# Two-layer hybrid decoder trunk on one core: branch products of the mixer in the score banks, two priorities, and three attention branches some pieces later

## The chip, the cores and the metric

The kernel runs on one core of a Trainium2 chip. The metric is device time in microseconds (us), the median of the runs shown. The engines are PE (TensorE), DVE (VectorE), ACT (ScalarE), POOL (GpSimd) and SP (SyncE, which issues the loads of weights). Matmul results land in PSUM, which is eight banks; a bank holds 512 float32 columns for each of 128 partitions.

## The reference

Two layers. Each is a SwiGLU feed-forward (FFN), a token mixer and a second FFN; after each of the three, `x = LayerNorm(ALPHA * x + (1 + gate) * F(modulate(x)))`. There are 256 tokens of width 1024. The mixer is the part that the change touches, cut to what matters:

```python
proj = u @ w_in                       # queries, keys, values of A, B, C, D; index; gate logits
y_a = dilated_window_attention(...)   # 3 groups x 2 heads, softmax
y_b = dsa_attention(...)              # top-64 keys of an index score, then softmax, 4 heads
y_c = stick_breaking_attention(...)   # 4 heads: exp(log_sigmoid(z) + reversed cumulative sum)
y_d = forgetting_attention(...)       # 4 heads: softmax of q k + a cumulative sum of log f
gates = sigmoid(g_logit + b_gate).reshape(b, t, 4, D)
merged = sum(gates[:, :, i] * (branches[i] @ w_branch[i]) for i in range(4))
return merged @ w_out
```

## The kernel before

**Matmuls.** Every float32 product is three passes over float32r halves: a weight is loaded as `raw`, ACT casts it to `hi` (L262), DVE subtracts to get `lo` (L267), and PE runs hi by hi, hi by lo and lo by hi (`split_mm`, L286 to L288 with the weight stationary, L290 to L292 with the activations stationary).

**Order.** The code is straight-line Python. A planner at build time turns it into one queue for each engine: it goes by program position, and takes the earliest instruction that its own model of time says is ready, so that a later matmul can be put ahead of one that would wait. `tc.high_priority(offset=n)` moves the instructions inside it n positions ahead in that ranking. On the chip each queue runs in its fixed order.

**The mixer as pieces.** A `tick()` follows each piece of projection work, and `plan()` hangs the attention steps on tick numbers with `on(n, step)`. Ticks 15 to 18 follow the four pieces of a value projection. From tick 23 on the gate projections run in sixteen groups, one for each of 4 branches and 4 pairs of output blocks (`gates(bi, (pr,))`, two ticks each, one per half); after each but the first comes the product of the group before (`branch(bi, pr)`) and one tick. So group g has the ticks 3g+22 and 3g+23, and the branch product of group g-1 stands ahead of tick 3g+24. The branches come in the order A, C, D, B.

**PSUM.** Three rings of banks: `mm` (2 banks, projections), `acc` (4 banks, `acc_bank()`: scores, sums of C, outputs `y` of attention, the final output) and `tp` (2 banks, `tp_bank()`: transposes, and here the branch products). A ring's bank is taken again when the last reader of its former content is done.

**Steps.** `c_scores(j)` makes two heads' scores of C in two `acc` banks each; DVE adds the mask (L923). `c_logs` is one long chain over all of C's scores: ACT (L931 to L933), DVE (L934), `lf` on POOL, `eh` on ACT (L938), `el` on DVE (L939). `c_sums(j)` (L949 to L952) reads `eh` and `el` into the two `acc` banks x and y, which DVE subtracts (L954, L955); ACT takes the exponential (L956). `d_scores(j)` needs eight small tiles `lb` that POOL makes from `lf` (L968), two `acc` banks (L971, L972, then L744) and ends in a softmax (DVE L789, ACT L791 and L795). `pair_pt` transposes the probabilities of two heads into two `tp` banks (L749 to L751), and ACT copies each to `pt` (L753). `pair_pv` multiplies by the values into one `acc` bank (L762, L765); `y_out` splits that into halves (ACT L778, DVE L779). `a_pt` and `a_pv` do the same for A (copy L899, product L905).

**Merging.** `branch` multiplies gate and product on DVE (L1069 for A, L1071 for the others) and adds to `merged` (L1073, on POOL for C and D, on DVE for B). After B the merged block is cast to `mh` (ACT L1077) and its remainder to `ml` (DVE L1078), and `out` multiplies by the output weights.

Of the kernel before, what the change touches and what calls it, by code (L numbers as in the profile page):

```python
# [11 lines left out]
F32 = mybir.dt.float32  # L12
F32R = mybir.dt.float32r
BF16 = mybir.dt.bfloat16
AF = mybir.ActivationFunctionType
ALU = mybir.AluOpType
PSUM = bass.MemoryType.PSUM

D = 1024
# [67 lines left out]
MP = (0,1,0,0)  # L87
RP = 500
PP = 500
CS = 3  # L90
CVV = 4
NA0 = 0,1,3
NA1 = 0,2
FREE = 4
# [50 lines left out]
def trunk(ctx: ExitStack, tc: tile.TileContext, x, xT, crow, ada0, adac, adab, w_in0, w_in0x, gcol, bcol, ln_g, ln_b,  # L145
          w_in, w_out, mpair, mv0, mv12, mbrA, mbr, mwo, bgate, bforget, eye, rot, masks, out):
    nc = tc.nc
# [22 lines left out]
    def acc_bank():  # L170
        return pacc.tile([P, 512], F32, tag="acc", name="acc")
# [4 lines left out]
    def tp_bank():  # L176
        return ptp.tile([P, 512], F32, tag="tp", name="tp")
# [70 lines left out]
    def load(*srcs):  # L248

        widths = [src.shape[-1] for src in srcs]  # L250
        halves = [n if n <= 1024 else n // 2 for n in widths]
        parts = [[] for _ in srcs]
        for o in range(2):
            for src, n, half, got in zip(srcs, widths, halves, parts):
                if o * half >= n:
                    continue
                with tc.high_priority(offset=HP):
                    raw = wp.tile([P, 1024], F32, tag="raw", bufs=RB, name="raw")
                    nc.sync.dma_start(raw[:, :half], src[:, o * half:(o + 1) * half])
                    hi, lo = w_pair()  # L260
                    with behind() if held["free"] <= 0 < held["left"] else ExitStack():
                        nc.scalar.copy(hi[:, :half], raw[:, :half])  # L262
                        if held.get("pool_lo"):
                            held["pool_lo"] -= 1
                            nc.gpsimd.tensor_sub(lo[:, :half], raw[:, :half], hi[:, :half].bitcast(F32))
                        else:
                            held["lo"] = nc.vector.tensor_sub(lo[:, :half], raw[:, :half], hi[:, :half].bitcast(F32)).ins  # L267
                    held["left"] -= 1
                    held["free"] -= 1
                    got.append((hi, lo))  # L270

        def getter(half, got):
            def get(off, w):
                hi, lo = got[off // half]
                off %= half
                return hi[:, off:off + w], lo[:, off:off + w]
            return get

        gets = [getter(h, g) for h, g in zip(halves, parts)]
        return gets[0] if len(gets) == 1 else gets  # L280

    def split_mm(ps, w, xh, xl, start, stop, w_stationary=True):

        wh, wl = w
        if w_stationary:
            nc.tensor.matmul(ps, lhsT=wh, rhs=xh, start=start, stop=False)  # L286
            nc.tensor.matmul(ps, lhsT=wh, rhs=xl, start=False, stop=False)  # L287
            nc.tensor.matmul(ps, lhsT=wl, rhs=xh, start=False, stop=stop)  # L288
        else:
            nc.tensor.matmul(ps, lhsT=xh, rhs=wh, start=start, stop=False)  # L290
            nc.tensor.matmul(ps, lhsT=xh, rhs=wl, start=False, stop=False)  # L291
            return nc.tensor.matmul(ps, lhsT=xl, rhs=wh, start=False, stop=stop).ins  # L292
# [346 lines left out]
    def mixer(l, u, nxt, steps):  # L639
# [12 lines left out]
        def on(n, *fs):  # L652
            turns.setdefault(n, []).extend(fs)

        def tick():
            at["n"] += 1
            for f in turns.pop(at["n"], []):
                f()
# [87 lines left out]
        def transposed(p0, p1):  # L746

            ps = tp_bank()
            nc.tensor.transpose(ps[:, 0:128], p0, ident)  # L749
            nc.tensor.transpose(ps[:, 128:256], p1[:, 0:128], ident)  # L750
            nc.tensor.transpose(ps[:, 256:384], p1[:, 128:256], ident)  # L751
            pt = sp.tile([P, 384], F32, tag="pt", bufs=PTB, name="pt")
            nc.scalar.copy(pt, ps[:, :384])  # L753
            return pt

        def pv(y, heads):
# [48 lines left out]
        def head_pt(p):  # L805
            return transposed(p[:, 0:128], p[:, 128:384])
# [79 lines left out]
        def a_blocks(t):  # L886

            return [(g, h, kt) for g in range(3) for kt in range(t + 1) for h in range(2)]

        def a_pt(t):  # L890
            blocks, p = a_blocks(t), live["A"]
            live["Ap"] = []
            for i in range(0, len(blocks), 3):
                ps = tp_bank()
                for b, (g, h, kt) in enumerate(blocks[i:i + 3]):
                    c = (h * 3 + g) * 128 * (t + 1) + kt * 128
                    nc.tensor.transpose(ps[:, b * 128:b * 128 + 128], p[:, c:c + 128], ident)
                pt = sp.tile([P, 384], F32, tag="pt", bufs=PTB, name="pt")
                nc.scalar.copy(pt, ps[:, :384])  # L899
                live["Ap"] += [pt[:, b * 128:b * 128 + 128] for b in range(3)]  # L900

        def a_pv(t):
# [74 lines left out]
        def plan():  # L977

            f = lambda g, *a: (lambda: g(*a))
            for n, h in ((A0T, 0), (A0T + AST, 1)):  # L980
                on(n, f(a_scores, h))
                on(n + 3, f(a_pt, h))
                on(n + 4, f(a_pv, h))
            on(IK, index_keys)
            for h in range(4):
                on(IK + 3 + h, f(index_scores, h))
            for n in range(IK + 7, IK + 23):
                on(n, f(topk, 1))
            on(IK + 24, chosen)
            for j in range(2):  # L990
                on(15 + j, f(c_scores, j))
            on(16, c_logs)
            for j in range(2):
                on(20 + CS + j, f(c_sums, j))
            for j in range(2):
                on(23 + CVV + j, f(pair_pv, "C", j, 3))
                on(26 + 6 * j, f(d_scores, j))
                on(38 + 6 * j, f(b_scores, j))
                on(29 + 6 * j, f(pair_pt, "D", j))
                on(30 + 6 * j, f(pair_pv, "D", j, 5))  # L1000
                on(41 + 6 * j, f(pair_pt, "B", j))
                on(42 + 6 * j, f(pair_pv, "B", j, 1))
            for n, t in enumerate(STEPS):
                on(t, step)
            for n, piece in enumerate(held["affine"]):
                def late(piece=piece):
                    with tc.issue_after(held["lo"]):
                        piece()
                on(AM + n, late)
# [5 lines left out]
        for i in range(3):  # L1015
            for j, p in enumerate(proj(mpair[l, i], 2)):
                (qa if 2 * i + j < 3 else ka).append(rope(p, "qa", -0.125) if 2 * i + j < 3 else rope(p, "ka"))
        at["n"] = 0
        plan()
        iq = [rope(p, "iq") for p in proj(mpair[l, 3], 2)]  # L1020
        vproj([mv0[l, 0], mv0[l, 1]], 456, 0, extra=72)
# [30 lines left out]
        def branch(bi, pr):  # L1052

            b, last = BR_ORDER[bi], bi == 3
            k0, nk = KO[b]
            if pr == 0:
                src = mbrA[l] if b == 0 else mbr[l, b - 1]
                wb[bi] = load(src.rearrange("p a b -> p (a b)"))
            ps = tp_bank()
            for j in range(2):  # L1060
                m = pr * 2 + j
                for k in range(nk):
                    split_mm(ps[:, j * 256:(j + 1) * 256], wb[bi](k * D + m * 128, 128), ys[k0 + k][0], ys[k0 + k][1],
                             k == 0, k == nk - 1)
            tick()
            t = tg[bi, pr].rearrange("p a b -> p (a b)")
            mg = merged[:, 2 * pr:2 * pr + 2].rearrange("p a b -> p (a b)")
            if bi == 0:
                nc.vector.scalar_tensor_tensor(mg, t, 1.0, ps, op0=ALU.add, op1=ALU.mult)  # L1069
            else:  # L1070
                nc.vector.scalar_tensor_tensor(t, t, 1.0, ps, op0=ALU.add, op1=ALU.mult)  # L1071
                eng = nc.vector if last else nc.gpsimd
                eng.tensor_tensor(mg, mg, t, op=ALU.add)  # L1073
            if last:
                hslice = mh[:, 2 * pr:2 * pr + 2].rearrange("p a b -> p (a b)")
                lslice = ml[:, 2 * pr:2 * pr + 2].rearrange("p a b -> p (a b)")
                nc.scalar.activation(hslice, mg, AF.Copy, scale=0.5)  # L1077
                nc.vector.scalar_tensor_tensor(lslice, mg, 0.5, hslice.bitcast(F32), op0=ALU.mult, op1=ALU.subtract)  # L1078


        todo = []
# [9 lines left out]
        while turns:  # L1091
            tick()
        branch(*todo.pop(0))

        accs = [acc_bank() for _ in range(4)]
# [96 lines left out]
```

## Time and profile before

| | before |
|---|---|
| median of 3 runs | 1311.38 us (1308.73 to 1312.22) |
| the profiled execution's own time | 1315.82 us |
| its span, first to last instruction | 1314.0 us |
| PE busy | 1265.7 us (96%) |
| DVE, ACT, POOL busy | 1036.5, 652.6, 142.8 us |
| granted TensorE clock, mean | 0.998 |
| mixer of layer 0, of layer 1 (about) | 215 to 465 us, 860 to 1110 us |

Busy time of PE counts overlapped matmuls, so 96% doesn't say that PE runs at its peak; the distances between the starts of matmuls, and the waits, say where it lost time.

### The profile page before, as it was taken

What the parts mean: (1) busy time and instruction counts of PE and PEld (TensorE: products, weight loads), DVE (VectorE), ACT (ScalarE), POOL (GpSimd) and SP (SyncE); (2) the same over time, 40 slices, a digit from 0 to 9 for tenths busy, and PEclk for the clock granted to TensorE, in tenths of its full rate; (3) what the DMA queues carried; (4) which work ended last, traced back from release to release, by engine and by line L of the source; (5) the groups of instructions that cost most, each with busy time, mean ns of one, the idle gap of its engine ahead of it and who ended that gap; (6) DMA issues with size and microseconds to landing.
All of it is one profiled execution on the core that took longest, in us unless ns stands there. A gap on an engine that the chain in (4) does not pass through costs nothing.

```text
span 1314.0 us, 23415 instructions
## 1 busy us (share of the span) xinstructions
PE 1265.7 (96%) x9178; PEld 1175.6 (89%) x9178; DVE 1036.5 (79%) x1701; ACT 652.6 (50%) x1023; POOL 142.8 (11%) x150
## 2 busy tenths in 40 slices
PE   6999999999999999999999999999999999999997
PEld 5989888989989889998989999899989898899995
DVE  7788887888786799877698877688878768976565
ACT  4554355447564554444355444354666545554440
POOL 0130000214222000000000000012060210100000
PEclk9999999999999999999999999999999999999999
DMA  9889893756665639887548987457476655585530
GB/s 341 324 285 313 302 306 141 255 185 223 225 235 181 227 127 319 302 277 262 175 147 312 311 282 248 128 171 239 163 248 232 222 182 175 215 315 193 187 135 33
DMA packets 85847, 300.42 MB, mean 229 GB/s; under 512 B 10604, under 2 KB 12316, under 8 KB 85736
## 3 DMA queue, kind: packets, MB, share of 16 engines
q1 hardware_dynamic: 84392, 298.00, 66.3%
q8 instruction: 72, 1.18, 0.4%
q10 hardware_dynamic: 576, 0.60, 0.1%
q0 software_dynamic: 768, 0.32, 0.1%
q14 instruction: 39, 0.32, 0.1%
HBM read 297.81 MB, written 1.07 MB: 227 GB/s over the span
## 4 chain that ended last, share of the span: by engine, by line
PE 43%; issue 19%; DMA 16%; DVE 15%; ACT 5%; POOL 1%; DVEq 0%; ACTq 0%; SPq 0%; POOLq 0%
PE mm L286 9%; PE mm L287 8%; PE mm L288 8%; DVE lo L267 6%; DMA raw<-in_w_in_dram 5%; DMA raw<-in_adac_dram 5%; PE acc L290 3%; PE acc L292 3%; PE acc L291 3%; ACT hi L262 3%; DMA raw<-in_w_out_dram 3%; DVE raw L308 3%; DMA raw<-in_mpair_dram 1%; PE tp L286 1%; PE mm L290 1%
## 5 line engine op out<-in xcount | busy, mean ns | idle before, releaser
L267 DVE TENSOR_TENSOR lo<-raw,hi 128x1024 fp32r<-128x1024 f32 (+2 forms) x421 | 508.1, 1222 | 161.3 <-ACT hi L262 159.2
L262 ACT CAST hi<-raw 128x1024 fp32r<-128x1024 f32 (+1 forms) x422 | 433.8, 1040 | 322.3 <-PE mm L287 126.9
L286 PE MATMUL mm<-uh,hi 128*128 128x256 f32 x2032 | 574.7, 283 | 5.3 <-DVE h L525 3.1
L287 PE MATMUL mm<-ul,hi 128*128 128x256 f32 x2032 | 571.2, 281 | 0.0
L288 PE MATMUL mm<-uh,lo 128*128 128x256 f32 x2032 | 570.6, 281 | 0.0
L286 PEld LDWEIGHTS mm<-uh,hi 128*128 128x128 f32 x2032 | 383.0, 189 | 12.2 <-issue 5.3
L287 PEld LDWEIGHTS mm<-ul,hi 128*128 128x128 f32 x2032 | 383.5, 189 | 1.3
L288 PEld LDWEIGHTS mm<-uh,lo 128*128 128x128 f32 x2032 | 383.1, 189 | 0.3
L308 DVE CUSTOM_DVE_ANT_0 raw<-raw,cond_row,adab 128x1024 f32<-128x1024 f32 x128 | 163.9, 1292 | 47.1 <-DMA raw<-in_adac_dram 47.0
L290 PE MATMUL acc<-hi,hh 128*128 128x512 f32 x352 | 140.6, 400 | 2.2 <-ACT hh L531 1.7
L291 PE MATMUL acc<-lo,hh 128*128 128x512 f32 x352 | 139.1, 395 | 0.8 <-DVE lo L267 0.8
L292 PE MATMUL acc<-hi,hl 128*128 128x512 f32 x352 | 137.6, 396 | 0.1
L290 PEld LDWEIGHTS acc<-hi,hh 128*128 128x128 f32 x352 | 66.1, 188 | 17.7 <-ACT hh L531 3.3
L531 ACT CAST hh<-h 128x256 fp32r<-128x256 f32 x82 | 33.2, 405 | 97.4 <-DVE h L525 95.7
L292 PEld LDWEIGHTS acc<-hi,hl 128*128 128x128 f32 x352 | 65.9, 187 | 17.1 <-DVE hl L532 0.6
L291 PEld LDWEIGHTS acc<-lo,hh 128*128 128x128 f32 x352 | 66.1, 188 | 15.0 <-DVE lo L267 1.1
L408 POOL TENSOR_TENSOR rstd<-rstd,nhalf 128x1 f32<-128x1 f32 x12 | 7.6, 634 | 479.8 <-DVE rstd L407 479.8
L532 DVE TENSOR_TENSOR hl<-h,hh 128x256 fp32r<-128x256 f32 x74 | 31.2, 421 | 12.6 <-ACT hh L531 12.6
L290 PE MATMUL acc<-hi,uh 128*128 128x256 f32 (+1 forms) x128 | 38.7, 303 | 1.5 <-ACT uh L436 1.4
L1073 POOL TENSOR_TENSOR merged<-merged,tg 128x512 f32<-128x512 f32 x16 | 24.8, 1548 | 135.7 <-DVE tg L1071 57.2
L286 PE MATMUL tp<-y,hi 128*128 128x256 f32 x112 | 33.2, 297 | 5.8 <-ACT pt L753 5.7
L292 PE MATMUL acc<-hi,ul 128*128 128x256 f32 (+1 forms) x128 | 38.3, 299 | 0.0
(242 smaller groups left out, 1519.7 us busy)
## 6 DMA issues: line engine op xcount, KB each, us to landing
raw<-in_w_in_dram SPq DMA_DIRECT2D x174, 512.0 KB, 5.5
raw<-in_adac_dram SPq DMA_DIRECT2D x128, 512.0 KB, 5.4
raw<-in_mpair_dram SPq DMA_DIRECT2D x104, 512.0 KB, 4.9
raw<-in_w_out_dram SPq DMA_DIRECT2D x88, 512.0 KB, 5.3
ada<-in_ada_dram SPq DMA_DIRECT2D x16, 512.0 KB, 6.7
raw<-in_mwo_dram SPq DMA_DIRECT2D x16, 512.0 KB, 4.5
raw<-in_mv_dram SPq DMA_DIRECT2D x16, 384.0 KB, 3.8
raw<-in_mbr_dram SPq DMA_DIRECT2D x12, 512.0 KB, 3.8
```

What stands on the lines that cost most here:

```text
L262: nc.scalar.copy(hi[:, :half], raw[:, :half])
L267: held["lo"] = nc.vector.tensor_sub(lo[:, :half], raw[:, :half], hi[:, :half].bitcast(F32)).ins
L286: nc.tensor.matmul(ps, lhsT=wh, rhs=xh, start=start, stop=False)
L287: nc.tensor.matmul(ps, lhsT=wh, rhs=xl, start=False, stop=False)
L288: nc.tensor.matmul(ps, lhsT=wl, rhs=xh, start=False, stop=stop)
L290: nc.tensor.matmul(ps, lhsT=xh, rhs=wh, start=start, stop=False)
L291: nc.tensor.matmul(ps, lhsT=xh, rhs=wl, start=False, stop=False)
L292: return nc.tensor.matmul(ps, lhsT=xl, rhs=wh, start=False, stop=stop).ins
L308: nc.vector.tensor_tensor_reduce(raw, raw, cond_row, 0.5, adab_sb[:, l * 3 + s, v, n:n + 1], ALU.mult, ALU.add, accum_out=t[:, n:n + 1])
L531: nc.scalar.copy(hh, h)
L532: eng.tensor_sub(hl, h, hh.bitcast(F32))
L1073: eng.tensor_tensor(mg, mg, t, op=ALU.add)
```

## The change

Four things in the mixer; no instruction is added or taken away, and no load.

- `branch` takes its bank from `acc` for the branches A, C and D (24 products in the two layers), and from `tp` as before for B (8 products).
- The four instructions that end a block of the last branch (multiply, add, `mh`, `ml`) stand under a priority of 600.
- The copies of transposes to `pt` (L753 and L899) stand under a priority of 400. The loads and casts of weights have 300 in both kernels.
- Tick numbers: `c_scores` and `c_logs` one later (15, 16 to 16, 17; 16 to 17), `c_sums` two later (23, 24 to 25, 26), the products of C one later (27, 28 to 28, 29), all steps of D one later, all steps of B two later.

```diff
-CS = 3
-CVV = 4
+CS = 5
+CVV = 5
+MGP = 600
+PTP = 400
...
-            nc.scalar.copy(pt, ps[:, :384])
+            with tc.high_priority(offset=PTP):
+                nc.scalar.copy(pt, ps[:, :384])
...
-                on(15 + j, f(c_scores, j))
-            on(16, c_logs)
+                on(16 + j, f(c_scores, j))
+            on(17, c_logs)
             for j in range(2):
                 on(20 + CS + j, f(c_sums, j))
             for j in range(2):
                 on(23 + CVV + j, f(pair_pv, "C", j, 3))
-                on(26 + 6 * j, f(d_scores, j))
-                on(38 + 6 * j, f(b_scores, j))
-                on(29 + 6 * j, f(pair_pt, "D", j))
-                on(30 + 6 * j, f(pair_pv, "D", j, 5))
-                on(41 + 6 * j, f(pair_pt, "B", j))
-                on(42 + 6 * j, f(pair_pv, "B", j, 1))
+                on(27 + 6 * j, f(d_scores, j))
+                on(40 + 6 * j, f(b_scores, j))
+                on(30 + 6 * j, f(pair_pt, "D", j))
+                on(31 + 6 * j, f(pair_pv, "D", j, 5))
+                on(43 + 6 * j, f(pair_pt, "B", j))
+                on(44 + 6 * j, f(pair_pv, "B", j, 1))
...
-            ps = tp_bank()
+            ps = tp_bank() if last else acc_bank()
...
+            elif not last:
+                nc.vector.scalar_tensor_tensor(t, t, 1.0, ps, op0=ALU.add, op1=ALU.mult)
+                nc.gpsimd.tensor_tensor(mg, mg, t, op=ALU.add)
             else:
-                nc.vector.scalar_tensor_tensor(t, t, 1.0, ps, op0=ALU.add, op1=ALU.mult)
-                eng = nc.vector if last else nc.gpsimd
-                eng.tensor_tensor(mg, mg, t, op=ALU.add)
-            if last:
...
+                with tc.high_priority(offset=MGP):
+                    nc.vector.scalar_tensor_tensor(t, t, 1.0, ps, op0=ALU.add, op1=ALU.mult)
+                    nc.vector.tensor_tensor(mg, mg, t, op=ALU.add)
+                    nc.scalar.activation(hslice, mg, AF.Copy, scale=0.5)
+                    nc.vector.scalar_tensor_tensor(lslice, mg, 0.5, hslice.bitcast(F32), op0=ALU.mult, op1=ALU.subtract)
```

## Rows read from the trace of the kernel before

**Rows 1.** The page: busy us of each engine, share of the span, instructions.
```profile
PE 1265.7 (96%) x9178; PEld 1175.6 (89%) x9178; DVE 1036.5 (79%) x1701; ACT 652.6 (50%) x1023; POOL 142.8 (11%) x150
```

**Rows 2.** PE's waits: who waits for whom, us in total, times, longest.
```profile
PE tp L286 <- ACT pt L753: 5.7, 7, 1.1
...
PE acc L292 <- DVE ml L1078: 2.8, 2, 1.6
PE acc L949 <- DVE el L939: 2.2, 2, 1.1
...
PE acc L921 <- DVE y L779: 1.4, 2, 0.8
...
PE acc L291 <- DVE lo L267: 0.8, 1, 0.8
```

**Rows 3.** Timeline of ACT, layer 0: start, us, engine, line, what, count.
```profile
334.00 1.64 ACT L795 ACTIVATE p<-p,su 128x128 f32<-128x128 f32 x4
...
335.79 2.00 ACT L262 CAST hi<-raw 128x1024 fp32r<-128x1024 f32 x2
...
338.41 0.86 ACT L753 COPY pt<-tp 128x384 f32<-128x384 f32 x2
```

**Rows 4.** Timeline of PE from D's first transposes on; in brackets the idle time before.
```profile
336.32 0.27 PE L749 MATMUL tp<-ident,p 128*128 128x128 f32 x1
...
336.89 0.36 PE L286 MATMUL mm<-uh,hi 128*128 128x256 f32 x1
...
338.28 0.28 PE L288 MATMUL mm<-uh,lo 128*128 128x256 f32 x1
...
338.95 0.39 PE L286 MATMUL tp<-y,hi 128*128 128x256 f32 x1 [0.39 <-ACT pt L753]
```

**Rows 5.** Timeline of PE in the output product, layer 0.
```profile
456.12 0.39 PE L291 MATMUL acc<-lo,mh 128*128 128x512 f32 x1
458.10 0.50 PE L292 MATMUL acc<-hi,ml 128*128 128x512 f32 x1 [1.59 <-DVE ml L1078]
```

**Rows 6.** Timeline of DVE from the last branch product to its last remainder, layer 0.
```profile
444.40 0.68 DVE L1071 SCALAR_TENSOR_TENSOR tg<-tg,tp 128x512 f32<-128x512 f32 x1
...
457.36 0.68 DVE L1078 SCALAR_TENSOR_TENSOR ml<-merged,mh 128x512 fp32r<-128x512 f32 x1
```

**Rows 7.** Timeline of DVE at the end of `c_logs`, layer 0.
```profile
311.37 2.35 DVE L267 TENSOR_TENSOR lo<-raw,hi 128x1024 fp32r<-128x1024 f32 x2
313.64 1.76 DVE L939 TENSOR_TENSOR el<-e,eh 128x1544 fp32r<-128x1544 f32 x1
```

**Rows 8.** Timeline of PE, layer 0: a value piece, then `c_sums(1)`, `d_scores(0)`, A's first product.
```profile
290.75 0.45 PE L290 MATMUL mm<-hi,uh 128*128 128x384 f32 x1
...
293.03 0.70 PE L921 MATMUL acc<-cq,ck 64*128 64x256 f32 x2
...
319.80 0.28 PE L952 MATMUL acc<-el,cr 128*128 128x256 f32 x1
...
325.71 0.34 PE L971 MATMUL acc<-cr,lb 128*128 128x384 f32 x1
...
326.29 0.34 PE L971 MATMUL acc<-cr,lb 128*128 128x384 f32 x1
...
327.83 0.39 PE L286 MATMUL tp<-y,hi 128*128 128x256 f32 x1
...
328.74 0.44 PE L762 MATMUL acc<-zm,V 128*64 128x256 f32 x2
```

**Rows 9.** Timeline of DVE after `c_sums(1)`, layer 0.
```profile
322.29 0.41 DVE L955 TENSOR_TENSOR zm<-zm,acc 128x256 f32<-128x256 f32 x1
322.62 0.67 DVE L954 TENSOR_TENSOR zm<-zm,acc 128x512 f32<-128x512 f32 x1
```

**Rows 10.** Timeline of POOL: the eight `lb` of `d_scores(0)`, layer 0.
```profile
313.78 10.72 POOL L968 TENSOR_SCALAR lb<-cr,lf 128x128 fp32r<-128x128 f32 x8
```

**Rows 11.** The instructions of L968: count, and shortest, median and longest in ns.
```profile
L968 POOL TENSOR_SCALAR lb<-cr,lf x32: 595/602/3165, 313.8 to 981.0; 128x128 fp32r<-128x128 f32 x32
```

More of the change, by code (lines that the diff above doesn't have):

```diff
@@ L898, in a_pt @@
                 pt = sp.tile([P, 384], F32, tag="pt", bufs=PTB, name="pt")
-                nc.scalar.copy(pt, ps[:, :384])
+                with tc.high_priority(offset=PTP):
+                    nc.scalar.copy(pt, ps[:, :384])
                 live["Ap"] += [pt[:, b * 128:b * 128 + 128] for b in range(3)]
@@ L1069, in branch @@
                 nc.vector.scalar_tensor_tensor(mg, t, 1.0, ps, op0=ALU.add, op1=ALU.mult)
-            else:
-                nc.vector.scalar_tensor_tensor(t, t, 1.0, ps, op0=ALU.add, op1=ALU.mult)
-                eng = nc.vector if last else nc.gpsimd
-                eng.tensor_tensor(mg, mg, t, op=ALU.add)
-            if last:
+            elif not last:
+                nc.vector.scalar_tensor_tensor(t, t, 1.0, ps, op0=ALU.add, op1=ALU.mult)
+                nc.gpsimd.tensor_tensor(mg, mg, t, op=ALU.add)
+            else:
                 hslice = mh[:, 2 * pr:2 * pr + 2].rearrange("p a b -> p (a b)")
                 lslice = ml[:, 2 * pr:2 * pr + 2].rearrange("p a b -> p (a b)")
-                nc.scalar.activation(hslice, mg, AF.Copy, scale=0.5)
-                nc.vector.scalar_tensor_tensor(lslice, mg, 0.5, hslice.bitcast(F32), op0=ALU.mult, op1=ALU.subtract)
+                with tc.high_priority(offset=MGP):
[3 more added lines that the diff above has]
+                    nc.vector.scalar_tensor_tensor(lslice, mg, 0.5, hslice.bitcast(F32), op0=ALU.mult, op1=ALU.subtract)
         todo = []
```

## The prediction

> **What bounds the kernel now.** I read the page first: PE is busy for 1265.7 us, 96% of the span, and no other engine comes near it over the whole; DVE has 79% [rows 1]. So a microsecond counts where PE has nothing to run, and nowhere else. The second view is therefore PE's waits. Five groups matter here [rows 2]: branch products wait for copies of transposes (seven times, 5.7 us), the output product for the last remainder `ml` (2.8), the sums of C for `el` (2.2), the scores of C for a bank that A's output still holds (1.4), and the halves of weights, which cost 0.8 us in a single wait, at 153 us in an FFN. The first four all lie in the two mixers and add up to 5.7 + 2.8 + 2.2 + 1.4 = 12.1 us.
>
> The third view, the timelines of PE, says what such a wait costs in all. Twelve matmuls of 256 columns start between 336.89 and 338.28 [rows 4], 0.116 us apart; the branch product behind them starts 0.67 us after the last: 0.55 lost for 0.39 of idle time shown. In the output product, with 512 columns and so 0.23 apart, the starts are 456.12 and 458.10 [rows 5]: 1.75 lost for 1.59 shown. Each wait thus costs 0.16 us beyond its idle time. With thirteen waits (7 + 2 + 2 + 2, [rows 2]) that is 13 x 0.16 = 2.1 us, and the four groups cost 14.2 us together.
>
> **Why the waits are there.** After D's first transposes PE runs those twelve matmuls of the next gate group and then stands before the branch product. That product needs one of two `tp` banks, both hold transposes, and ACT, after a softmax (to 335.64), took two casts of weights in 2.00 us and two gate activations before the copies, which ran from 338.41 to 339.27 [rows 3]. The queue was fixed in the expectation that the copy is done a little sooner than it is. The last merge has the same fault on DVE: the multiply of the last product starts at 444.40, the remainder `ml` starts at 457.36 [rows 6], so four instructions of 0.7 us each take 13.6 us because weights' subtractions for the next FFN stand between them. And `el` (1.76 us) stands behind two such subtractions of 2.35 us [rows 7].
>
> **Part 1, products in `acc` banks, and D and B a piece later.** No instruction changes its length. The 24 products no longer ask for a bank that a transpose holds, so the wait of 5.7 us at that place goes by construction, with 7 x 0.16 = 1.1 us behind it. The next reader of the copies is the values' product (L762). It stood right behind the branch product; now a half gate piece lies between. Its length: two halves run between 319.80 and 325.71 [rows 8], so 2.9 us each. Even in the old ACT order the copies ended 339.27 - 336.89 = 2.4 us after the transposes [rows 3, 4], which leaves 0.5 us; with the priority they start after at most the cast that is running. I take 0 for the new wait and keep 5.7 as the other end.
>
> **Part 2, priority for the copies.** ACT does the same 28 copies, 0.43 us apart in pairs [rows 3]; casts and gate activations behind a pair come 0.86 us later. What hides that: PE waits for halves of weights once, and not in the mixer [rows 2], and ACT is busy for 50% [rows 1]. Without that cover 14 pairs would cost 14 x 0.86 = 12 us. I take 0.
>
> **Part 3, priority for the last merge.** The four instructions of a block, 0.7 us each by [rows 6], then run one after the other, in about 3 us from 444.40: `ml` is there by 448, 10 us before PE asks at 458. All of 2.8 + 2 x 0.16 = 3.1 us goes. The subtractions for the next FFN come 1.4 us later; PE needs those only after the layer's end. Nothing new is put on DMA queues.
>
> **Part 4, C later.** `c_scores(0)` now stands a value piece after A's product, 293.03 - 290.75 = 2.3 us [rows 8], against a wait of at most 0.8 [rows 2]: 1.4 + 0.3 goes. `c_logs` starts at most 2.3 us later, less the 1.0 just gained, and `c_sums` two half gate pieces later, 5.8 us, against a wait of 1.1: 2.2 + 0.3 goes. No moved step issues a DMA: the loads of condition columns hang on tick numbers of their own, which stay, and weights come with their pieces in the same order on SP's queue. On POOL the store of a gate row stands behind the `lb` tiles; that row is read at the layer's end, over 100 us later.
>
> **What is late next.** Before, two half pieces (5.9 us) lay between `c_sums(1)` and `d_scores(0)` [rows 8]. Now only A's first product does, 328.74 - 327.83 = 0.9 us [rows 8], and that takes an `acc` bank too. `c_sums` holds four banks; the two of j = 0 are free by then, and go to the product and to D's first head. The second head, 0.6 us later (325.71 to 326.29, [rows 8]), needs one that DVE has to release after `c_sums(1)`. The release took long before: last matmul from 319.80 to 320.08, the smaller subtraction done at 322.69, the larger at 323.29 [rows 8, 9], so 2.6 and 3.2 us. Cover is 0.9 + 0.6 = 1.5. The new wait is 2.6 - 1.5 = 1.1 us in each layer, 2.2 in all. The ends: nothing, if the queue has gate matmuls ahead of that head, as after the transposes in [rows 4], and 3.2 us in each layer without cover. I take 1.1, since the first bank released suffices.
>
> The eight `lb` tiles stand at the same place. They are done at 324.50 [rows 10], 1.8 us before D's second head starts at 326.29 [rows 8]. PE comes 1.3 us sooner (2.2 us of waits gone, 0.9 of product put ahead) and `lf` up to 1.0 later, which makes a wait of at most 0.5 us, within the 1.1. Alone such a tile takes 0.60 us, at worst 3.17 [rows 11], and the eight took 10.72 in place of 4.8 [rows 10]. The Trainium skill, "SBUF — State Buffer", section "Who interferes with whom", has a rule that fits these rows: a GpSimd instruction that reads SBUF and a DVE instruction with two inputs there need one port pair, and the later one blocks until the first ends. By it a `lb` that meets DVE's subtractions more often costs more, against this change; that is the last rival below.
>
> **The sum.** -14.2 + 2.2 = -12.0 us. The profiled execution took 1315.82 us, 0.3% more than the median of 1311.38; it would come to 1303.8, and the median to **1299.4 us**. What follows the mixer starts from the last output matmul, and weights keep PE waiting for 0.8 us in the whole kernel [rows 2], so nothing there takes the gain back.
>
> **Rivals.**
> Transposes late: the softmax of D ended at 335.64, 0.7 us before the first transpose at 336.32 [rows 3, 4]. C's subtractions now fall in that softmax: two pairs of 1.0 us on DVE [rows 9]. If both stand ahead, the transposes wait 2.0 - 0.7 = 1.3 us in each layer, and with the restart and two more places of that size about 5 us: 1304. For it speaks how often this trace misses by about 1 us; against it, that PE's queue can run gate matmuls first.
> The change does not do what it says: the wait goes from the branch product to the values' product. Then 5.7 + 1.1 us stay, 14.2 - 6.8 - 2.2 = 5.2 are gained: 1306.2. For it: only 0.5 us of slack in the old ACT order. Against: the priority.
> No change that can be measured: 0.3%, 3.9 us, is about what tells a gain from none here. New waits must then eat 10 us, ten of the 1 us size that this trace has; the transposes, both banks at their upper end (6.4 us) and a few more could: about 1310.
> Slower: POOL's `lb` tiles under DVE's subtractions. To lose 3.9 us the waits at `d_scores(0)` must reach 14.2 + 3.9 = 18.1, 9 us in each layer; with 0.5 already due, the eight would take 10.7 + 8.5 = 19.2 us, 2.4 each against 1.34 now [rows 10]. It stays within what a single one took (3.17). At that point: 1315.3. Against it: few of DVE's instructions would have to move to make a mean of nearly twice the old one.
>
> **How the numbers follow.** My forecast 0.60, transposes late 0.16, values' product 0.09, no change 0.10, slower 0.05. The first three are faster by over 0.3%, but for 0.02 at their edge: faster 0.83, same 0.12, slower 0.05. Range: all 14.2 us gone and nothing new gives 1297.2, and runs scatter by 2 us or so: from 1295; upward to the values' product and half of the way to no change: to 1308. The likeliest case alone: 1295 to 1303.
>
> **What the profile will show.** Right: no wait of L286 for L753, none of L292 for L1078; `ml` ends within 4 us of the last multiply; waits of L949 and L921 below 0.3 us; a wait of about 1 us before L971 or L744 in each mixer, released by L955, L954 or L968. Wrong: L762 waiting for L753; L749 waiting for L795; weights' casts (L262, L267) ahead of PE in the mixer; or a `d_scores(0)` that waits 3 us or more.

## Result: the four waits went, two larger ones came, and the clock fell behind them

The changed kernel takes 1327.1 us (median of 4 runs, 1322.24 to 1330.72), the one before 1311.8 (4 runs, 1308.73 to 1313.28). The ratio is 1.0121 [1.0089, 1.0154]: slower by about 15 us, where 12 us faster was forecast. The profiled execution, the fastest of the four, has a span of 1320.5 us at a mean clock of 0.991, against 1314.0 at 0.998.

The waits of PE after the change, to be read beside [rows 2] (total, times, longest, in us; line numbers are two to six higher than before):

```profile
core 0 of [0], span 1320.5 us
engine line waited for: us in total, times, longest us
PE tp L288 <- ACT uh L339: 12.5, 1, 12.5
PE acc L975 <- DVE zm L958: 10.9, 2, 5.8
PE mm L428 <- DVE x L420: 6.5, 7, 1.3
PE tp L751 <- ACT p L798: 2.9, 2, 1.6
PE hT L611 <- DVE h L609: 2.5, 3, 1.1
PE acc L288 <- DVE zm L959: 1.4, 2, 1.2
PE tp L752 <- ACT p L798: 1.3, 2, 1.0
```

The groups of `pt`, `ml`, `el` and `y` are gone, as forecast. In their place stands D's second head (L975), which waits for a score bank that a subtraction of C's sums (L958) has to release: the place and the releaser that the prediction named, with 5.1 and 5.8 us where it had 1.1. The transposes' wait for the probabilities `p` is new, and the transposes of `x` at the boundaries between the parts of a layer (L428) wait seven times instead of five.

**How the second head came to wait.** The timeline of PE there, layer 0 (start, duration, engine, line; in brackets the idle time before):

```profile
317.63 0.28 PE L956 MATMUL acc<-el,cr 128*128 128x256 f32 x1
318.07 0.39 PE L288 MATMUL acc<-y,hi 128*128 128x256 f32 x1 [0.15 <-DVE zm L959]
...
320.64 0.28 PE L289 MATMUL mm<-ul,hi 128*128 128x256 f32 x1
...
321.34 0.28 PE L289 MATMUL mm<-ul,hi 128*128 128x256 f32 x1
326.72 0.66 PE L975 MATMUL acc<-cr,lb 128*128 128x384 f32 x1 [5.10 <-DVE zm L958]
...
330.01 0.41 PE L288 MATMUL mm<-uh,hi 128*128 128x256 f32 x1
...
333.00 0.41 PE L290 MATMUL mm<-uh,lo 128*128 128x256 f32 x1
```

The sums' last matmul starts at 317.63, as 319.80 did before [rows 8]. Then the timeline of DVE over the same stretch:

```profile
317.60 0.41 DVE L959 TENSOR_TENSOR zm<-zm,acc 128x256 f32<-128x256 f32 x1
317.93 0.68 DVE L958 TENSOR_TENSOR zm<-zm,acc 128x512 f32<-128x512 f32 x1
322.41 1.29 DVE L310 CUSTOM_DVE_ANT_0 raw<-raw,cond_row,adab 128x1024 f32<-128x1024 f32 x1 [3.81 <-DMA raw<-in_adac_dram]
...
323.62 2.36 DVE L269 TENSOR_TENSOR lo<-raw,hi 128x1024 fp32r<-128x1024 f32 x2
325.90 0.68 DVE L958 TENSOR_TENSOR zm<-zm,acc 128x512 f32<-128x512 f32 x1
326.50 0.41 DVE L959 TENSOR_TENSOR zm<-zm,acc 128x256 f32<-128x256 f32 x1
```

The two subtractions at the top belong to `c_sums(0)`, the two at the bottom to `c_sums(1)`. Between them DVE's fixed order has a reduction of condition columns (L310) and two weights' subtractions (L269). The reduction waits 3.81 us for its load; with it and the weights' subtractions 3.5 us of work come first, and the subtraction of the sums, which could have run from 318.6 on, starts at 325.90. From the last matmul's end (317.91) to the first release (326.58) it is 8.7 us, where [rows 8, 9] have 2.6. The same reduction was late before too, but there it stood behind both subtractions [rows 9] and one of a weight. The next rows of DVE in the kernel before:

```profile
324.09 1.26 DVE L267 TENSOR_TENSOR lo<-raw,hi 128x1024 fp32r<-128x1024 f32 x1 [0.79 <-ACT hi L262]
328.17 1.28 DVE L308 CUSTOM_DVE_ANT_0 raw<-raw,cond_row,adab 128x1024 f32<-128x1024 f32 x1 [2.82 <-DMA raw<-in_adac_dram]
```

No wait of PE hung on it there. It is the fifth reduction for the `shift` columns, the first of the step on tick 34: the gate's steps have ticks 5 to 20, those on 25 and 30 make reductions one to four. The planner puts a reduction where it expects the load to be there, not at its tick. With the sums two ticks later, DVE's order has four of them ahead of the first sums and the fifth between the two; before it had three and the fourth, whose load had landed. In layer 1 the same stands at 973.46, after 4.47 us (before: 972.82, after 4.08 us, and behind both subtractions).

**What the stop did to the clock.** Windows of 3 us of the changed kernel (length; busy us and count of PE, PEld, DVE, ACT, POOL; granted clock, DMA share, GB/s):

```profile
318.00:321.00 3.00, 2.93 (x19) 2.41 (x20) 0.61 (x2) 3.00 (x6) 1.38 (x3) 1.00 1.01 410
321.00:324.00 3.00, 0.62 (x6) 0.41 (x4) 1.59 (x3) 1.10 (x3) 0.02 (x1) 1.00 0.33 132
324.00:327.00 3.00, 0.28 (x1) 0.31 (x2) 3.00 (x5) 0.06 (x1) 2.96 (x4) 0.59 0.61 198
327.00:330.00 3.00, 3.00 (x9) 2.02 (x9) 1.32 (x8) 1.67 (x5) 3.00 (x6) 0.50 0.86 295
330.00:333.00 3.00, 3.00 (x16) 3.00 (x15) 2.78 (x9) 2.48 (x8) 0.42 (x1) 0.50 0.30 57
333.00:336.00 3.00, 3.00 (x20) 2.07 (x19) 0.67 (x3) 0.37 (x1) 0.00 (x0) 0.70 0.72 257
```

The clock stands at its upper level (2.4 GHz) up to 324.54 by the trace's clock records, while PE stands since 321.62, and then at the lower one (1.2 GHz) for 2.46 + 6.0 + 1.8 = 10.2 us: from the shares, (1 - 0.59) x 3 / 0.5 and so on. So PE worked in 10.2 - (326.72 - 324.54) = 8.0 of them. Gate matmuls start 0.214 us apart there (14 steps from 330.01 to 333.00) and 0.117 before the stop (6 steps from 320.64 to 321.34), so 45% of this time, an estimated 3.6 us, is lost behind the stop itself. In layer 1 the lower level lasts 6.8 us, from 976.48; PE starts again at 977.77, works in 5.5 of them, and 2.5 are lost by the same estimate.

**The account.** From the starts of PE's instructions I take the two mixers from the last transpose of the boundary ahead to the last one of the boundary behind: 523.1 us before, 535.5 after, so +12.4 where -12.0 was forecast. The 24.4 us between them: the second head 10.9 - 2.2 = 8.7; the clock 3.6 + 2.5 = 6.1; waits that came elsewhere, `p` 2.9 + 1.3, the first product's for `zm` 1.4, `x` 6.5 - 3.9 = 2.6 (the 3.9 are the wait of L426 for `x` before), 8.2 together; and restarts, eight more waits (4 + 2 + 2) of 0.16, 1.3. That is 24.3. It closes less well than it looks: the wait for `qa` (L678, 2.1 us in two, in the mixers before) has also gone, which with its restarts leaves about 22 us, and 2.4 unexplained. What lies outside the two mixers took 791.0 us in the profiled execution before and 785.0 after; over the sixteen profiled executions it lies between 785.0 and 792.3, without any order by version. So the spans differ by 6.5 us only, where the mixers differ by 12.4 and the medians by 15.

### The profile page after: what moved, and what is told of

It reads as the page before. It is cut to its first block, busy times and chain, and to the rows that moved or that the text cites. A ratio compares the mean times of both kernels' runs of the same rounds, so it can differ in the third digit from the quotient of the medians.

```text
span 1320.5 us, 23418 instructions
## 1 busy us (share of the span) xinstructions
PE 1270.8 (96%) x9178; PEld 1179.8 (89%) x9178; DVE 1039.1 (79%) x1701; ACT 655.1 (50%) x1023; POOL 144.1 (11%) x150
## 5 line engine op out<-in xcount | busy, mean ns | idle before, releaser
L269 DVE TENSOR_TENSOR lo<-raw,hi 128x1024 fp32r<-128x1024 f32 (+2 forms) x421 | 508.3, 1220 | 170.3 <-ACT hi L264 168.0
L310 DVE CUSTOM_DVE_ANT_0 raw<-raw,cond_row,adab 128x1024 f32<-128x1024 f32 x128 | 163.6, 1290 | 37.2 <-DMA raw<-in_adac_dram 37.2
L524 ACT ACTIVATE th<-mm 128x256 f32<-128x256 f32 x74 | 27.9, 377 | 24.9 <-PE mm L290 24.7
```

The costliest lines, as they stand in the source:

```text
L310: nc.vector.tensor_tensor_reduce(raw, raw, cond_row, 0.5, adab_sb[:, l * 3 + s, v, n:n + 1], ALU.mult, ALU.add, accum_out=t[:, n:n + 1])
L524: nc.scalar.activation(th, pg, AF.Tanh, scale=0.5)
```

## Experiments

Fourteen runs beside the kernel before, each time on the same chip. In the expectations of the first runs, where "the step on tick 25" is named, it is held for the owner of the late reduction; as shown above it is that on tick 34.

**Three ways to take the collision away.** The sums of C back to ticks 23 and 24, all else as in the changed kernel:

```
-CS = 5
+CS = 3
```


> The changed kernel with the sums of C back on ticks 23 and 24 (all other moves kept). Theory A expects the release well ahead of D's scores: no wait at L975, clock 1.0; but the wait of the sums for el may come back, up to 2.5 us in all, more than before because the chain that makes el starts a piece later. About 1305 to 1311. If the loss came from the other moves (products in acc, B two pieces later, the priorities), the time stays at about 1325.

The first product back in a transposes' bank, so that the second head has one bank more:

```
-            ps = tp_bank() if last else acc_bank()
+            ps = tp_bank() if last or (bi, pr) == (0, 0) else acc_bank()
```


> The changed kernel with A's first product alone back in a tp bank (2 of the 24 products of the two layers). D's two heads then find the two banks of c_sums(0) and need none of c_sums(1). Theories A and B both expect no wait for L958 at D's scores (under 0.5 us), a clock of 1.0 in the mixers, and about 1306 to 1310, with the reductions where they are in the changed kernel. Rival C (lb on POOL, or DVE late in general) expects the wait to stay at 5 us in each layer.

A step of condition columns later:

```
-STEPS = (5, 10, 15, 20, 25, 30, 34, 37, 40, 43, 46, 49, 52, 54)
+STEPS = (5, 10, 15, 20, 27, 30, 34, 37, 40, 43, 46, 49, 52, 54)
```


> The changed kernel with one step of the condition columns (two loads and two reductions on DVE) hung on tick 27 in place of 25, so that DVE has both subtractions of c_sums(1) ahead of those reductions. Theory A: the 5.1 and 5.8 us that D's second head waited were the time in which DVE stood before a reduction whose load had not landed; then the wait at L975 falls from 10.9 us to about 2 (1.1 in each layer, as first forecast), the clock stays at 1.0 through both mixers, and the time is some 15 us below the changed kernel, about 1311. Rival B: four banks are too few for two sums, a product and two heads, whoever releases them; then at least 3 us are left in each layer and the clock still falls. Rival C: the lb tiles on POOL are what is late; then the wait stays.

Measured: 1314.02 (ratio 1.0024 [1.0004, 1.0045]), 1312.37 (1.0009 [0.9993, 1.0025]) and 1312.11 (1.0014 [0.9993, 1.0034]). Each takes back the loss, the first all but 0.2% of it, and none gains; the first two stay above the times expected of them (1305 to 1311, 1306 to 1310). In each, a wait stands at the next place where PE meets DVE or ACT, and in the first and the third the clock is at its lower level for 3.4 us in each mixer, where it was expected to stay up. With the sums early, the late reduction is still late but stands behind both subtractions:

```profile
318.39 0.41 DVE L959 TENSOR_TENSOR zm<-zm,acc 128x256 f32<-128x256 f32 x1
...
323.79 1.28 DVE L310 CUSTOM_DVE_ANT_0 raw<-raw,cond_row,adab 128x1024 f32<-128x1024 f32 x1 [3.85 <-DMA raw<-in_adac_dram]
```

SP's queue has the same order here as in the changed kernel, so this run keeps the late load and only brings the sums ahead of it: the head no longer waits. It is the softmax that comes late for the transposes. With the first product in its old bank, the values' product of C (L765) waits for the same subtraction:

```profile
...
PE tp L751 <- ACT p L798: 7.6, 4, 2.5
PE mm L428 <- DVE x L420: 6.6, 7, 1.3
```

(the sums early), and

```profile
...
PE mm L428 <- DVE x L420: 6.8, 7, 1.5
PE acc L765 <- DVE zm L958: 5.3, 2, 2.7
PE tp L751 <- ACT p L798: 3.1, 3, 1.4
PE tp L752 <- ACT p L798: 2.3, 2, 1.7
```

(the first product in its old bank). With the step later, the reduction comes behind the subtractions as well, and the first product waits 5.4 us in two.

**The load or the place in the queue.** First the loads of tick 25's step were issued on tick 22, in the belief that they were the late ones:

```
+            on(22, lambda: early.update({(l, 2, 0, n): fetch_cols(l, 2, 0, n) for n in range(2)}))
...
-                nc.sync.dma_start(raw, adac[l, s, v, n])
+                raw = early.pop((l, s, v, n), None) or fetch_cols(l, s, v, n)
```


> The changed kernel, with the two condition-column loads of the step on tick 25 issued on tick 22 and their reductions left on tick 25. DVE's queue around the sums' subtractions keeps its order (two reductions, two casts, subtractions); only the load comes some four weight loads earlier. If the order of the queue and a late landing make the collision: the idle 3.8 and 4.5 us of DVE ahead of the reductions go, D's second head waits 0 to 1.5 us instead of 5.1 and 5.8, the granted clock stays at its upper level there, and the time is 1311 to 1315. If the traffic of the stretch (321 to 331 GB/s) sets the pace: the two weight loads that now come behind land later, the casts in front of the subtractions wait for them instead, D's second head still waits 4 us or more and the time is 1322 or more.

1323.82 us, 1.011 [1.0092, 1.0128]. Read by its expectation alone this run speaks for the traffic. Its trace says otherwise: DVE idles ahead of the same reduction, whose load kept its place in SP's queue behind four loads of weights, and the head waits 5.88 us in layer 0 (line numbers here are six higher again):

```profile
319.83 0.68 DVE L964 TENSOR_TENSOR zm<-zm,acc 128x512 f32<-128x512 f32 x1
325.08 1.28 DVE L316 CUSTOM_DVE_ANT_0 raw<-raw,cond_row,adab 128x1024 f32<-128x1024 f32 x1 [4.57 <-DMA raw<-in_adac_dram]
...
326.29 2.35 DVE L269 TENSOR_TENSOR lo<-raw,hi 128x1024 fp32r<-128x1024 f32 x2
328.57 0.68 DVE L964 TENSOR_TENSOR zm<-zm,acc 128x512 f32<-128x512 f32 x1
```

The run moved the wrong load, and so did not test what it was made for; it showed which reduction is the late one. The next moves that one:

```
-STEPS = (5, 10, 15, 20, 25, 30, 34, 37, 40, 43, 46, 49, 52, 54)
+STEPS = (5, 10, 15, 20, 25, 30, 37, 38, 40, 43, 46, 49, 52, 54)
```


> The changed kernel with the step on tick 34 on tick 37 and that on 37 on 38, nothing else. The reduction that stands between the two sums' subtractions in DVE's queue of the changed kernel is the first of the step on tick 34 (the fifth pair of loads of the mixer after the gate's four); with its step moved, it comes behind the second sums' subtraction. If the order of DVE's queue makes the collision: no idle of 3 us or more of DVE ahead of that subtraction, D's second head waits under 2 us in each layer, the clock stays up there, and the time is 1310 to 1316. If the cause is the score bank and the traffic whatever the order: D's second head waits 4 us or more in each layer and the time is 1321 or more.

1313.36 us, 1.0014 [0.9997, 1.0031]. Only the ticks of two steps differ from the changed kernel, and 14 us are back. A step's loads move with it, so this run alone doesn't part the load from the place in DVE's queue; the sums put early do, with the load as late as ever and no loss. The head's wait is halved and not gone, so the "under 2 us" was too low:

```profile
319.61 0.68 DVE L958 TENSOR_TENSOR zm<-zm,acc 128x512 f32<-128x512 f32 x1
322.12 1.23 DVE L269 TENSOR_TENSOR lo<-raw,hi 128x1024 fp32r<-128x1024 f32 x1 [1.84 <-ACT hi L264]
323.27 0.41 DVE L959 TENSOR_TENSOR zm<-zm,acc 128x256 f32<-128x256 f32 x1
```

A weight's subtraction (L269) stands ahead of that of the sums, and waits in its turn for a cast on ACT. The wait is 2.5 us in each layer. In layer 0 the clock stays at its upper level. In layer 1, where the first product also waits 2.1 us, 3.7 us earlier, it is at the lower one for 6.8 us, which was not expected.

**The parts alone.** The later ticks alone (products in the transposes' banks, no new priority); the products of A, C and D in the score banks alone; the copies' priority alone; the last merge's priority alone:

```
-            ps = tp_bank() if last else acc_bank()
+            ps = tp_bank()
...
-MGP = 600
-PTP = 400
+MGP = 0
+PTP = 0
```


> The changed kernel with its later ticks alone: all branch products in the transposes' banks and no new priority, as before. If the collision needs both the late sums and a product that takes a score bank: D's second head waits under 1 us, the values' product of C waits some 2.7 us in each layer as it did with the first product moved back, the waits for copies of transposes (5 to 6 us) and of the last merge (3 us) are there as before, and the time is 1311 to 1316. If the late ticks alone make it: D's second head waits 5 us in each layer, and the time is 1325 or more.

```
-            ps = tp_bank()
+            ps = tp_bank() if last else acc_bank()
```


> The kernel before with the products of A, C and D in the score banks, all else as before. If the bank alone does no harm while the sums come on ticks 23 and 24, and gains what the removed waits for a transposes' bank were worth at most: 1308 to 1312, the waits of y and el go or halve, D's second head waits under 1.5 us. If the shorter supply of score banks is itself the cost: D's second head or the first product waits 3 us or more in each layer, and the time is 1316 or more.

```
-            nc.scalar.copy(pt, ps[:, :384])
+            with tc.high_priority(offset=400):
+                nc.scalar.copy(pt, ps[:, :384])
```


> The kernel before with the priority of the copies of transposes alone. If PE is held only by the copies: the value products' wait for pt (5.7 us in seven) falls below 1 us and the time is 1304 to 1307. If the softmax behind them is the pace: pt's wait goes and 3 us or more of waiting for p or another tile comes in its place, time 1308 to 1312.

```
+                with tc.high_priority(offset=MGP):
+                    nc.scalar.activation(hslice, mg, AF.Copy, scale=0.5)
+                    nc.vector.scalar_tensor_tensor(lslice, mg, 0.5, hslice.bitcast(F32), op0=ALU.mult, op1=ALU.subtract)
```
(and the multiply and the add ahead of these, for the last branch)


> The kernel before with the priority for the last merge alone. By the working of the prediction the wait for ml (2.8 us and 0.3 us of restart) goes and nothing comes in its place: 3.1 us, about 1308.7. Rival: the layer's end waits elsewhere instead (the transposes of the boundary for x, which the changed kernel shows at 6.5 us against 3.9), and the time stays at 1311.8.

The last three and none of the first together:

```
-CS = 5
-CVV = 5
+CS = 3
+CVV = 4
...
-                on(27 + 6 * j, f(d_scores, j))
+                on(26 + 6 * j, f(d_scores, j))
```
(and the other ticks of `plan` back in the same way)


> The changed kernel with every tick put back where it was: products of A, C and D in the score banks, priority of the copies and of the last merge, and nothing later. If the waits that go can be added up as the prediction did it: the pt group (5.7 us) and the ml group (2.8 us) go, with their restarts 9.9 us, el and y stay, and the time is 1300 to 1304. If a removed wait comes back at the next place where PE meets DVE or ACT: pt and ml are gone from the list, at least 6 us of others stand in their place (the boundary's x, the values' product, the softmax), and the time is 1308 to 1312.

Measured: ticks alone 1316.21 (1.0052 [1.0033, 1.0071]), banks alone 1311.17 (1.0015 [0.9999, 1.0032]), copies alone 1310.43 (0.9993 [0.9979, 1.0008]), merge alone 1310.74 (1.0005 [0.9988, 1.0023]), the three together 1310.80 (1.0003 [0.9986, 1.002]). So the late ticks cost some 7 us by themselves, at the upper edge of what was expected of them, with a wait of the values' product of C (5.4 us in two, longest 3.2); the waits for copies of transposes, expected to stay, are down to 1.2, and the transposes wait 5.6 for `p` instead. With the banks alone the wait for `y` goes, that for `el` stays (2.4), and the values' product asks for `pt` (3.1 in five). With the merge's priority alone `ml` goes and `x` is up to 5.9 in seven, as its rival had it. No other part does anything that can be measured, alone or with the rest. The three together, which by the prediction's way of adding should be worth 9.9 us:

```profile
...
PE mm L428 <- DVE x L420: 5.8, 7, 1.3
PE acc L765 <- ACT pt L756: 4.8, 6, 1.1
...
PE acc L953 <- DVE el L943: 2.1, 2, 1.1
```

PE no longer stands before the branch product (5.7 us in seven) but before the values' product behind it (4.8 in six). `ml` (2.8 in two) is gone and `x` is up from 3.9 in five to 5.8 in seven. The copies' priority explains itself: with it alone, the queues of PE, DVE, ACT, POOL and SP all stand in the order of before. It moved nothing, so neither of its two expectations could come, and the wait of the branch product is 5.0 us in seven where it was 5.7:

```profile
...
PE tp L286 <- ACT pt L754: 5.0, 7, 1.1
```

That run is thus the kernel before once more, and shows what two single traces of one order differ by: 521.1 us in the mixers against 523.1, and 0.8 us of waiting for `qa` against 2.1.

**Giving the softmax time.** If the waits only wander because PE comes too early, more of PE's other work ahead of the transposes should keep some of the gain. On top of the first product in its old bank and tick 25's step on 27, D's and B's transposes and value products a tick later:

```
-                on(30 + 6 * j, f(pair_pt, "D", j))
-                on(31 + 6 * j, f(pair_pv, "D", j, 5))
-                on(43 + 6 * j, f(pair_pt, "B", j))
-                on(44 + 6 * j, f(pair_pv, "B", j, 1))
+                on(31 + 6 * j, f(pair_pt, "D", j))
+                on(32 + 6 * j, f(pair_pv, "D", j, 5))
+                on(44 + 6 * j, f(pair_pt, "B", j))
+                on(45 + 6 * j, f(pair_pv, "B", j, 1))
```


> The changed kernel with the step of tick 25 on tick 27, the first branch product back in a transposes' bank, and the transposes and value products of D and B one tick later (31 and 32, 44 and 45, each plus 6). If the waits of the three undo runs are matters of place that one more tick of other products covers: the transposes' wait for the probabilities falls from about 5 us to under 1.5, and the time is 1302 to 1308. If DVE, ACT and the loads set the pace of this stretch and PE only waits at the next place: the sum of PE's waits in it stays within 3 us of that of the undo runs, and the time is 1309 to 1314.

On this, the sums a tick earlier and B's value products a tick later again:

```
-CS = 5
+CS = 4
...
-                on(45 + 6 * j, f(pair_pv, "B", j, 1))
+                on(46 + 6 * j, f(pair_pv, "B", j, 1))
```


> The combination run before (tick 25's step on 27, first product in a transposes' bank, transposes and value products of D and B one tick later) with the sums of C a tick earlier (24, 25) and the value products of B a tick later again (46, 52). If bank and order are all that is left at D's second head: its wait falls from 3.9 us in both layers together to under 1.5, the wait for pt from 3.7 to under 1, and the time is 1302 to 1307. If the stretch is paced by DVE, ACT and loads, the waits come back elsewhere and the time is 1307 to 1311.

Or D's scores a tick later in place of the sums a tick earlier, with B's value products on 46 too:

```
-                on(27 + 6 * j, f(d_scores, j))
+                on(28 + 6 * j, f(d_scores, j))
```


> The same combination with the sums of C on 25 and 26 and D's scores a tick later (28, 34) instead, transposes of D three ticks behind them. If bank and order are all that is left: D's second head waits under 1.5 us, the transposes' wait for p stays under 1.5, and the time is 1302 to 1307. If the softmax is then late for the transposes again: p waits of 3 us or more and 1308 to 1312.

And the run with the sums a tick earlier, without the priority of the last merge:

```
-MGP = 600
+MGP = 0
```


> The fastest combination so far without the priority of the last merge. If that priority only moves its wait to the boundary's transposes: the ml wait of 2 to 3 us is back, the boundary's x falls from 5.8 to about 4, and the time is within 2 us of the combination with it, 1306 to 1310. If it is worth its removed wait: 1309 to 1312.

Measured, in this order: 1309.06 (0.9987 [0.9971, 1.0002]); 1307.37 (0.9961 [0.9948, 0.9975]); 1309.06 (0.9983 [0.9969, 0.9996]); 1307.38 (0.9976 [0.9955, 0.9997]). In the first the wait for `p` is gone, as expected, but the second head waits 3.9 us and the values' products 3.7 for `pt`, and the time is that of its second theory. The second run is faster than both kernels, by 0.4% than the one before. Its two mixers take 517.0 us against 523.1, by the same cut as above. The third waits 6.3 us for `p`, as its second theory has it. Without the merge's priority the second run's mixers take 518.4, `ml` is back with 4.4 us in two and `x` is down from 5.8 in seven to 3.5 in five: the priority carries the wait over the layer's end. The expectation that the second head's wait for a bank would go was met in the second run (none in its list), but the probabilities are late again:

```profile
...
PE tp L751 <- ACT p L798: 6.4, 4, 2.5
PE mm L428 <- DVE x L420: 5.8, 7, 1.3
```

## Why the prediction was wrong

**The step that failed** is the price of the second head: "The release took long before: [...] so 2.6 and 3.2 us. Cover is 0.9 + 0.6 = 1.5. The new wait is 2.6 - 1.5 = 1.1". The cover was 3.7 us (317.91 to 321.62) and not 1.5, since the first head's own scores and eight gate matmuls stand ahead of that head; such matmuls the prediction allowed for at its lower end. The 2.6 us is the release in the old order of DVE's queue; the change moved the sums past a reduction that the trace of before already showed standing 2.82 us for its load, just behind them. It became 8.7 us. 8.7 less 3.7, and 0.1 from the release to the start, is the wait of 5.1 seen. Two runs show it: putting the sums ahead of that reduction, with its load as late as before, took the ratio from 1.0121 to 1.0024, and moving its step took it to 1.0014, some 14 us. Two ends were given there, nothing and 3.2 us; the upper one took the old release too, and so held nothing new that could come ahead of the subtraction. "No moved step issues a DMA" was true, and beside the point: a step moved past another's DMA wait takes it over.

**The clock** had no term. A stop of 5.1 and one of 5.8 us cost an estimated 3.6 and 2.5 us more in the work behind them. The signs of error named "a `d_scores(0)` that waits 3 us or more"; that sign came.

**The four removed waits** went, as forecast. That they "cost 14.2 us together" was wrong as a gain. Without the second head's long wait the versions come to 1307 to 1316. With the old ticks the prediction's second rival was the true one for `pt`: the wait moves to the values' product. Its argument against it, the priority, fell: that wait is 4.8 us in six with the priority (the three parts together) and 3.1 in five without (the banks alone). In the changed kernel, with D and B a piece later, no values' product waits for `pt`, so there Part 1 held. That "nothing there takes the gain back", said of the layer's end, failed too: with the three parts `x` takes 1.9 us of `ml`'s 2.8. In the changed kernel the first rival holds in part, with 4.2 us of waiting for `p` against the 5 it priced, but at B's transposes and not D's. There ACT has casts of weights between the softmax's steps:

```profile
373.68 1.03 ACT L264 CAST hi<-raw 128x1024 fp32r<-128x1024 f32 x1
374.62 0.40 ACT L798 ACTIVATE p<-p,su 128x128 f32<-128x128 f32 x1
374.92 0.82 ACT L1049 ACTIVATE tg<-mm,hb 128x256 f32<-128x256 f32 x2
375.63 1.04 ACT L264 CAST hi<-raw 128x1024 fp32r<-128x1024 f32 x1
376.57 1.20 ACT L798 ACTIVATE p<-p,su 128x256 f32<-128x256 f32 x3
```

The transposes ask from 375.87 on. That DVE, ACT and the loads are the pace of this stretch altogether is argued only; the combinations, which do the same instructions in another order and won up to 0.4% of the time, speak against a fixed pace.

**Smaller readings** that were off without bearing on this: the last merge took 4.8 us from its multiply to the end of `ml` (446.80 to 451.55 in layer 0) and not about 3, which was still early enough; and the halves of weights had kept PE waiting three times before (0.8, 0.3 and 0.2 us, none in a mixer), not once.

**The slower rival** named the wrong engine. The eight `lb` tiles of POOL ended at 318.7 (11.3 us, against 10.72 in [rows 10]), 2.9 us before PE stopped. The tiles themselves were slowed: in the trace before, the 13 of the 32 that began while DVE was in an instruction with two inputs in SBUF (L267, L308, L939) took 1.31 to 3.17 us, the other 19 took 0.59 to 0.60. The trace thus agrees with the Trainium skill's rule on the shared port ("SBUF — State Buffer", "Who interferes with whom"), which costs PE nothing here, since nothing waited for the tiles. The subtractions of C's sums, which have one input in PSUM, are not among those that slowed a tile.

**Open in part** is why the ticks alone cost 7 us, while the same ticks with both priorities and all products of A, C and D but the first in score banks cost 1 (0.9993 to 1.0025). The two traces differ by some 5 us in the mixers, 526.0 against 521.2: PE's waits there add up to 19.1 us against 17.0, and behind a stop of 3.2 us in layer 1 the clock is at its lower level for 6.8 us, an estimated 2.6 us of lost work by the share above. Why the one stop was followed by that and the other version's stops of 2.6 and 2.7 us were not, no run shows.

## What to carry to other kernels

Before a step is moved along a fixed queue, look in the old trace at what that queue waits for on both sides of it, out to as far as it moves: an idle stretch that harmed nobody becomes the price of whatever lands behind it. A wait of about 1 us that is taken from an engine which is only just fed was worth nothing here until the next meeting with the same producers had slack, so price the next two meetings before adding waits up. And test whether a priority changes the queue's order at all: here one did not.

## What was not expected of the hardware

A stop can cost more than its length, and the length doesn't say how much. In the sixteen traces PE stands twenty times for 2.0 to 2.8 us after the kernel's start: eleven of these stops were followed by 3.4 us at a granted clock of 1.2 GHz, three by 6.8 us (two of the three, 3.7 us apart, share one such stretch), and six by none. The five longer stops were followed by 6.8 us (3.2 and 5.8 us of standing) or by 10.2 (4.0, 5.1 and 5.9 us).
